# The mask of the forgetful heads: from matmuls to additions on VectorE, with three pieces of the schedule moved

## The chip, the cores and the metric

The kernel runs on one core of a Trainium2 chip. The metric is the device time of one execution in microseconds; the time before is the median of three executions. The core has a matrix engine (TensorE, PE in the profile), two engines for elementwise work and reductions that can read the matrix engine's accumulator banks (VectorE, DVE; ScalarE, ACT), a general engine (GpSimd, POOL) and a sequencer that issues most DMAs (SP).

## What is computed

One layer of a streaming encoder on 1024 tokens of width 1024, all in float32: a normalised input goes through one wide projection into three mixers, whose outputs are gated, added and projected, and then through a gated MLP with a causal convolution.

```python
u = rms_norm(x, norm_mix_g) @ w_in          # latent, forgetting, scan and gate columns
y_a = latent_attention(u_mla) @ w_br_mla    # 8 heads, chunk-causal mask
y_b = forgetting_attention(u_fox) @ w_br_fox
y_c = scan_branch(u_ssm) @ w_br_ssm         # Mamba-2 state-space scan, 16 heads
g = sigmoid(u_gate + b_gate)                # three gates of width 1024
x = x + (g0 * y_a + g1 * y_b + g2 * y_c) @ w_out
x = x + conv_ffn(rms_norm(x, norm_ffn_g), ffn_w_up, ffn_conv_w, ffn_conv_b, ffn_w_down)
```

In forgetting attention the scores of query and key get the difference of two running sums of a forget gate, and keys after the query are masked out one by one:

```python
F = cumsum(log_sigmoid(f_raw + b_f))
s = q @ k.T * scale + F[query] - F[key]
p = softmax(where(key <= query, s, -inf))
```

## The kernel before

A float32 product is computed as three matmuls of a rounded high part and a low remainder (high by high, high by low, low by high). A helper, `split` (line 131), makes the two parts: the high part by a copy on ScalarE, the low one by a subtraction on VectorE.

The work runs in stages: the projections of the latent branch and of the forgetting and z columns (to about 387 us), attention, the scan, the three branch projections, the output projection, and the MLP. Two long lists of work cross the stages:

- **The fill** (`all_fill`, line 1162): the projection of the convolved columns and of the gates, 36 blocks of 48 matmuls (line 1179) on PE. It has no place of its own. `merge(streams, fill_us)` (line 1216) interleaves generators by a planned clock: each yields after a few matmuls with their planned cost, and the stream that is furthest behind its share goes next; `fill_us` says how much fill goes along, with three matmuls counted as 0.65 us. Steps on other engines are put into a queue with `later(us, fn)` (line 1076) and issued when the planned clock passes their due time. PE follows the order that is written out; the other engines' order is planned by a scheduler on that program, except for instructions that `pin` or `keep_in_program_order` ties. What fill is left after the scan is run out at once ahead of the branches.
- **Weight sums of the down projection** (`down_sums`, line 931): the last MLP product uses a scheme with seven block products, for which sums of weight blocks are prepared. Each call loads two tiles by SP, makes four sums on POOL and leaves two stores, which the next call or `down_flush` issues. Six calls are made in the early projections, five in the branches.

Attention (from line 1424): 16 heads, eight latent and then eight forgetting ones, four units each. A unit takes two rows of 128 queries. `score_row` (line 1282) computes the scores of a row in one or two chunks into banks of PSUM (three banks), three matmul passes for latent heads, two for forgetting ones. Then `finish` orders the rest of the row: `last_max` on VectorE (the negated maximum, line 1312, and for two chunks the smaller of two, line 1314), the exponential on ScalarE with its sum (line 1319), sum and reciprocal on VectorE (lines 1324 and 1325), and scaling on POOL (line 1326). The transposes of the probabilities (line 1384), their split and the products with the values (lines 1349 to 1357) come two units later.

The mask of the forgetting heads concerns the last 128 columns of a row. It is one more matmul into the bank of scores, a bf16 identity by a bf16 mask (line 1310), accumulated after the score matmuls. For these heads `finish` is not called in place: it goes into the list `held`, and `merge` or the next row calls it (`flush`), by preference just before the transposes of the values' stream (`tp_next`).

The scan (from line 1465) works on eight chunks of 128 tokens. `ssd_a` transposes the inputs (line 1506), transposes B and multiplies C by B into one bank (lines 1517 and 1519), copies and splits B's transpose (line 1520), makes `cbm` (line 1522) on VectorE from the same bank, and then the decay matrices E: differences by a Relu on ScalarE (line 1538), an exponential (line 1539), a product with `cbm` (line 1540). `ssd_b` makes states and outputs (lines 1548 and 1574) and the norm; `ssd_c` transposes the result (line 1609) and stores it. Fill runs between them, by `FILL_SSD` per chunk and 6.0 us ahead of the first.

The branches (from line 1678): forgetting first, then latent, then scan, each in eight column blocks of 128 (line 1729). A block loads its weights (line 1060) and its gates (line 1720) and splits the weights. The first two inputs of the forgetting branch are loaded into tiles (`ws0`, `ws1`) which the calls of `down_sums` in the branches use later.

Of the kernel before, what the change touches and what calls it, by code (L numbers as in the profile page):

```python
# [11 lines left out]
F32 = mybir.dt.float32  # L12
F32R = mybir.dt.float32r
BF16 = mybir.dt.bfloat16
I32 = mybir.dt.int32
AF = mybir.ActivationFunctionType
# [5 lines left out]
P = 128  # L22
# [20 lines left out]
def block_kernel(ctx: ExitStack, tc: tile.TileContext, x, positions, norm_mix_g, w_in, b_gate,  # L43
# [23 lines left out]
    def const(shape, dt, name):  # L67
        return (cp if name in keep else cp2).tile(shape, dt, name=name, tag=name)

    def scratch(shape, name, dt=F32):  # L70
# [22 lines left out]
    make_identity(nc, ident)  # L93
    identb = const([P, P], BF16, "identb")
    G.tensor_copy(identb, ident)
    ones = const([P, P], F32, "ones")
# [6 lines left out]
                    pattern=[[-1, P]], channel_multiplier=1)  # L103
    mfox = const([P, P], BF16, "mfox")
    G.memset(mfox, 0.0)
# [1176 lines left out]
    def score_row(o, i, pn):  # L1282
        flush()
        n = i + 1
# [6 lines left out]
        for ci, (a, b) in enumerate(chunks):  # L1291
            ps, pl = a_s.get()
            w = max(b - a, 256)
            last = ci == len(chunks) - 1
            for i_, (q_, k_) in enumerate(o.passes):
                T.matmul(ps[:, :w], q_[:, qs], k_[:, a:a + w], start=i_ == 0,  # L1296
                         stop=(o.br == 0 or not last) and i_ == len(o.passes) - 1)
            c = len(o.passes) * w / 2400
            pss.append((ps, pl))
            if not last:  # L1300
                later(c + 0.1, lambda ps=ps, ci=ci, a=a, b=b: pin(V.reduce_max(
                    nmx[:, ci:ci + 1], ps[:, :b - a], axis=AX, negate=True)))
                yield c
# [3 lines left out]
        def finish(t0=0.0):  # L1307

            if o.br == 1:
                T.matmul(ps[:, b - a - P:b - a], identb, mfox, start=False, stop=True)  # L1310
            def last_max():
                V.reduce_max(nmx[:, ci:ci + 1], ps[:, :b - a], axis=AX, negate=True)  # L1312
                if two:
                    V.tensor_tensor(nmx[:, 2:3], nmx[:, 0:1], nmx[:, 1:2], op=ALU.min)  # L1314
# [14 lines left out]

        if o.br == 0:  # L1330
            finish(c)
            yield c
        else:
            held.append(finish)
            yield c + 0.05

# [87 lines left out]
    with ExitStack() as pt__:  # L1424
# [10 lines left out]
        with tc.manual_schedule(engines={mybir.EngineType.PE}):  # L1435
# [6 lines left out]
            for n in range(len(units) + 2):  # L1442
# [11 lines left out]
                if n >= 2:  # L1454
# [4 lines left out]
                    st.append((me[0], cost_v(done[n - 2][1])))  # L1459
                merge(st, FILL_ATT * share)  # L1460
            flush()
# [12 lines left out]
    with ExitStack() as ps__:  # L1474
# [22 lines left out]
        def ssd_a(o, c):  # L1497
# [20 lines left out]
            for g in range(2):  # L1518
                T.matmul(pt[:, 2 + g, :], o.bc[:, g, :], o.bc[:, 2 + g, :], start=True, stop=True)
            split(*o.bT, pt[:, 0:2, :])  # L1520
            split(*o.c_, o.bc[:, 2:4, :])
# [12 lines left out]
            for q in range(4):  # L1534
                E = pool.tile([P, 4, P], F32, name=uid("E"), tag="E", bufs=4)
                for hh in range(4):
                    h = 4 * q + hh
                    A.activation(E[:, hh, :], o.row[:, h, :], AF.Relu, scale=-1.0, bias=cumc[:, c, h:h + 1])
                A.activation(E, E, AF.Exp, scale=-1.0)
                V.tensor_mul(E, E, cbm[:, q // 2:q // 2 + 1, :].to_broadcast([P, 4, P]))  # L1540
                o.E.append(E)
                if q == 1 and c + 1 < NT:
                    split(*o.xdd, xdd)
                yield 0.0
# [71 lines left out]
        with tc.manual_schedule(engines={mybir.EngineType.PE}):  # L1616
# [3 lines left out]
            load_rows(obj[0], 0)  # L1620
            merge([], 6.0)
            grain[0] = 4
# [15 lines left out]
    with ExitStack() as pe_:  # L1638
# [39 lines left out]
        for b, wsrc, nk in ((1, w_br_fox, 4), (0, w_br_mla, 4), (2, w_br_ssm, 8)):  # L1678
# [28 lines left out]
            for j in range(NK):  # L1707
                if (b, j) in ((1, 4), (0, 0), (2, 1), (2, 3), (2, 5)):
                    down_sums(ws_tiles())
                elif (b, j) in ((0, 3), (2, 6)):  # L1710
                    down_flush()
# [502 lines left out]
```

## Time and profile before

| | us |
|---|---|
| median of 3 runs | 2002.59 (2002.17 to 2005.0) |
| the profiled execution's own time | 2003.73 |
| its span, from the first instruction to the last | 2002.0 |
| PE busy | 1977.5 (99% of the span) |
| VectorE busy | 1365.9 (68%) |
| ScalarE busy | 944.5 (47%) |
| GpSimd busy | 651.9 (33%) |

Busy time of PE counts matmuls whose modelled spans overlap, so a full row does not say that it runs at its peak; the distance from one start to the next says what an instruction takes of the queue. A row of the timeline has start, duration, engine, line, operation, output and inputs, shapes, and in brackets the engine's idle time before it with what ended it. A row of the groups has the count, the busy time, the mean duration in ns, and the idle time before. A row of waits has who waited for whom, the total, how often, and the longest. "issue" stands where the profile shows no releaser.

### The profile page before, as it was taken

How to read it: one execution, taken by the hardware profiler on the slowest of the kernel's cores; microseconds unless marked ns; L12 is line 12 of the kernel's file. 1: busy time of each engine (PE TensorE's matmuls, PEld its weight loads, DVE VectorE, ACT ScalarE, POOL GpSimd, SP SyncE). 2: the span in 40 equal slices, each digit the busy share in tenths (PEclk: the TensorE clock that was granted, in tenths of full speed). 3: DMA queues.
4: the chain of work that ended last, by engine and by line, in shares of the span. 5: the costliest groups of instructions: out<-in, count | busy, mean ns of one | idle time of the engine just before them, and what ended most of it. 6: DMA issues, size and time to landing. Idle time of an engine off the chain costs nothing.

```text
span 2002.0 us, 28702 instructions
## 1 busy us (share of the span) xinstructions
PE 1977.5 (99%) x10185; PEld 1676.7 (84%) x10185; DVE 1365.9 (68%) x2345; ACT 944.5 (47%) x1778; POOL 651.9 (33%) x636
## 2 busy tenths in 40 slices
PE   8999999999999999999999999999999999999998
PEld 7989888888888888888888888888888888888887
DVE  7777567267666677656885476568997777666665
ACT  5555323255555556557775132225454444544432
POOL 5133322021212223213331252100764544423764
PEclk9999999999999999999999999999999999999999
DMA  5166857543535444427654786433332211249575
GB/s 178 52 195 210 277 179 224 165 125 105 139 114 145 122 120 133 125 78 238 183 192 139 259 284 202 144 119 107 104 95 90 78 55 53 78 159 337 188 262 185
DMA packets 278265, 312.18 MB, mean 156 GB/s; under 512 B 19197, under 2 KB 209289, under 8 KB 278122
## 3 DMA queue, kind: packets, MB, share of 16 engines
q1 hardware_dynamic: 278120, 310.35, 49.6%
q8 instruction: 80, 1.31, 0.3%
q14 instruction: 63, 0.52, 0.1%
q10 hardware_dynamic: 2, 0.00, 0.0%
HBM read 217.17 MB, written 93.13 MB: 155 GB/s over the span
## 4 chain that ended last, share of the span: by engine, by line
PE 86%; DVE 4%; issue 3%; DMA 3%; POOL 2%; ACT 2%; SPq 1%; ACTq 0%; DVEq 0%; POOLq 0%
PE mm L1179 19%; PE fx L798 9%; PE dn L2161 8%; PE ybr L1729 7%; PE ua L1820 6%; PE uc L1820 5%; PE ud L1820 4%; PE wo L1865 4%; PE s L1296 4%; PE tp L1384 3%; PE ub L1820 2%; PE fxv L188 2%; PE py L1574 1%; PE o L1357 1%; PE ckv L517 1%
## 5 line engine op out<-in xcount | busy, mean ns | idle before, releaser
L1326 POOL TENSOR_SCALAR pm<-pm,rs 128x128 f32<-128x128 f32 (+7 forms) x128 | 105.3, 826 | 413.9 <-DVE rs L1325 290.1
L1179 PE MATMUL mm<-hnh,wh 128*128 128x512 f32 x576 | 236.9, 411 | 0.0
L1179 PE MATMUL mm<-hnh,wl 128*128 128x512 f32 x576 | 226.0, 392 | 0.0
L1179 PE MATMUL mm<-hnl,wh 128*128 128x512 f32 x576 | 225.8, 392 | 0.0
L2161 PE MATMUL dn<-dr,dr 128*128 128x512 f32 x592 | 182.3, 389 | 0.0
L1319 ACT ACTIVATE pm<-s,nmx 128x128 f32<-128x128 f32 (+2 forms) x192 | 110.4, 581 | 64.9 <-DVE nmx L1314 61.4
L2161 PEld LDWEIGHTS dn<-dr,dr 128*128 128x128 f32 x592 | 111.1, 188 | 23.0
L1179 PEld LDWEIGHTS mm<-hnh,wl 128*128 128x128 f32 x576 | 108.1, 188 | 24.6
L1179 PEld LDWEIGHTS mm<-hnl,wh 128*128 128x128 f32 x576 | 108.9, 189 | 15.6
L1179 PEld LDWEIGHTS mm<-hnh,wh 128*128 128x128 f32 x576 | 108.8, 189 | 15.5
L1390 DVE TENSOR_TENSOR ptl<-tp,pth 128x512 fp32r<-128x512 f32 (+1 forms) x160 | 98.4, 633 | 32.8 <-ACT pth L1389 30.7
L1389 ACT ACTIVATE pth<-tp 128x512 fp32r<-128x512 f32 (+1 forms) x160 | 84.8, 555 | 72.6 <-PE tp L1384 72.5
L2161 PE MATMUL dn<-dr 128*128 128x512 f32 x296 | 115.3, 389 | 1.1 <-DVE dY L2178 1.1
L135 DVE TENSOR_TENSOR dr<-dr,dr 128x1024 fp32r<-128x1024 f32 x52 | 75.8, 1465 | 49.1 <-ACT dr L134 47.2
L1729 PE MATMUL ybr<-ah,wl 128*128 128x512 f32 x256 | 99.7, 390 | 1.1 <-DVE wl L135 1.1
L1729 PE MATMUL ybr<-al,wh 128*128 128x512 f32 x256 | 99.8, 390 | 0.0
L1729 PE MATMUL ybr<-ah,wh 128*128 128x512 f32 x256 | 99.7, 389 | 0.0
L134 ACT ACTIVATE dr<-dr 128x1024 fp32r<-128x1024 f32 x52 | 55.1, 1061 | 73.0 <-PE dn L2161 50.0
L1312 DVE TENSOR_REDUCE nmx<-s 128x1 f32<-128x384 f32 (+3 forms) x128 | 65.8, 518 | 32.7 <-PE s L1296 19.1
L134 ACT ACTIVATE wh<-wr 128x1024 fp32r<-128x1024 f32 (+1 forms) x40 | 35.1, 877 | 98.1 <-PE ybr L1729 45.9
L1384 PE MATMUL tp<-ident,pm 128*128 128x128 f32 x576 | 79.8, 273 | 0.6 <-POOL pm L1326 0.6
L135 DVE TENSOR_TENSOR wl<-S,wh 128x1024 fp32r<-128x1024 f32 x42 | 63.2, 1504 | 23.3 <-ACT wh L134 23.3
(531 smaller groups left out, 5782.7 us busy)
## 6 DMA issues: line engine op xcount, KB each, us to landing
dr<-act_d SPq DMA_DIRECT2D x99, 256.0 KB
wr<-in_w_in_dram SPq DMA_DIRECT2D x36, 512.0 KB
g_d<-t SPq DMA_DIRECT2D x24, 512.0 KB
gl<-g_d SPq DMA_DIRECT2D x24, 512.0 KB
wr<-in_ffn_w_up_dram SPq DMA_DIRECT2D x23, 512.0 KB
ws<-in_ffn_w_down_dram SPq DMA_DIRECT2D x22, 512.0 KB
wsum_d<-ws SPq DMA_DIRECT2D x22, 512.0 KB
act_d<-fa SPq DMA_DIRECT2D x22, 512.0 KB
```

The lines of the kernel that those rows point to most:

```text
L134: i = A.activation(h, src, AF.Copy) if he is A else he.tensor_copy(h, src)
L135: return i, le.tensor_sub(l, src, f32(h))
L798: T.matmul(p, a(k), b(k), start=k == 0 and i == 0, stop=k == NK - 1 and i == 2)
L1179: T.matmul(ps, a[:, k, :], b[half][:, k, :], start=(k == 0 and i == 0), stop=(k == NK - 1 and i == 2))
L1319: pss[cj][1][0] = later(t0 + 0.9 + 0.1 * cj, lambda cj=cj, a_=a_, b_=b_: A.activation(p_[:, a_:b_], pss[cj][0][:, :b_ - a_], AF.Exp, bias= ...
L1326: G.tensor_scalar(p_[:, 0:n * P], p_[:, 0:n * P], rs[:, 3:4], 0.0, op0=ALU.mult, op1=ALU.add)
L1384: T.transpose(pt[:, off:off + P], pn[qi][0][:, k * P:k * P + P], ident)
L1389: later(cs + 0.05, lambda th=th, pt=pt, off=off: A.activation(th[:, :off], pt[:, :off], AF.Copy))
L1390: pl[0] = later(cs + 0.6, lambda th=th, tl=tl, pt=pt, off=off: V.tensor_sub(tl[:, :off], pt[:, :off], f32(th[:, :off])))
L1729: T.matmul(pss[half], w_[:, k, :], a_[k][:, hs], start=k == 0 and i == 0, stop=k == nk - 1 and i == 2)
L1820: T.matmul(ps, a, b, start=first and n == 0, stop=n == 11, skip_group_check=not first)
L2161: T.matmul(ps[m], a[:, ts_], b[:, 512:], start=first_ and j == 0 and q == 0, stop=j == NFH - 1 and q == 2, skip_group_check=not first_)
```

## The change

The mask becomes a float32 tile, and the bf16 identity goes. Every row calls `finish` in place, whatever the kind of head; for forgetting heads `last_max` first adds the mask on VectorE to the last 128 columns, in PSUM. (`held` stays in the code and is always empty.) Three places of the schedule change with it. The first two units of attention get 2.0 us more fill each, and the scan's start gets 9.0 us of fill instead of 6.0. In the scan, each difference of a chunk is ordered behind the copy of B's transpose on ScalarE, an order without a semaphore. Two calls of `down_sums` move: from block 4 of the forgetting branch and block 0 of the latent one to blocks 2 and 6 of the forgetting branch; the flush in the latent branch comes at block 2 instead of 3.

```diff
-    identb = const([P, P], BF16, "identb")
-    G.tensor_copy(identb, ident)
...
-    mfox = const([P, P], BF16, "mfox")
+    mfox = const([P, P], F32, "mfox")
...
             for i_, (q_, k_) in enumerate(o.passes):
                 T.matmul(ps[:, :w], q_[:, qs], k_[:, a:a + w], start=i_ == 0,
-                         stop=(o.br == 0 or not last) and i_ == len(o.passes) - 1)
+                         stop=i_ == len(o.passes) - 1)
...
         def finish(t0=0.0):
 
-            if o.br == 1:
-                T.matmul(ps[:, b - a - P:b - a], identb, mfox, start=False, stop=True)
             def last_max():
+                if o.br == 1:
+                    V.tensor_add(ps[:, b - a - P:b - a], ps[:, b - a - P:b - a], mfox)
                 V.reduce_max(nmx[:, ci:ci + 1], ps[:, :b - a], axis=AX, negate=True)
...
-        if o.br == 0:
-            finish(c)
-            yield c
-        else:
-            held.append(finish)
-            yield c + 0.05
+        finish(c)
+        yield c
...
-                merge(st, FILL_ATT * share)
+                merge(st, FILL_ATT * share + (2.0 if n < 2 else 0.0))
...
-            split(*o.bT, pt[:, 0:2, :])
+            b_copy, _ = split(*o.bT, pt[:, 0:2, :])
...
-                    A.activation(E[:, hh, :], o.row[:, h, :], AF.Relu, scale=-1.0, bias=cumc[:, c, h:h + 1])
+                    behind_(A.activation(E[:, hh, :], o.row[:, h, :], AF.Relu, scale=-1.0, bias=cumc[:, c, h:h + 1]),
+                            b_copy)
...
-            merge([], 6.0)
+            merge([], 9.0)
...
-                if (b, j) in ((1, 4), (0, 0), (2, 1), (2, 3), (2, 5)):
+                if (b, j) in ((1, 2), (1, 6), (2, 1), (2, 3), (2, 5)):
                     down_sums(ws_tiles())
-                elif (b, j) in ((0, 3), (2, 6)):
+                elif (b, j) in ((0, 2), (2, 6)):
                     down_flush()
```

## The prediction

> **What bounds the kernel now.** I read the page first: busy shares, then the chain that ended last.
>
> ```profile
> span 2002.0 us, 28702 instructions
> PE 1977.5 (99%) x10185; PEld 1676.7 (84%) x10185; DVE 1365.9 (68%) x2345; ACT 944.5 (47%) x1778; POOL 651.9 (33%) x636
> PE 86%; DVE 4%; issue 3%; DMA 3%; POOL 2%; ACT 2%; SPq 1%; ACTq 0%; DVEq 0%; POOLq 0%
> ```
>
> TensorE is the bound: a microsecond is won only where a matmul leaves its queue or a wait of its queue goes. Next came the busy time by stage (columns: window, its length, then PE, PEld, DVE, ACT, POOL busy) for latent attention (387 to 634 us) and forgetting attention (634 to 886), and then PE's own waits from 386 to 1200 us.
>
> ```profile
> 387.00:634.00 247.00, 243.96 (x1421) 212.99 (x1420) 162.28 (x379) 134.11 (x335) 56.40 (x69) 1.00 0.46 124
> 634.00:886.00 252.00, 251.77 (x1506) 210.67 (x1505) 172.85 (x405) 145.18 (x360) 62.31 (x71) 1.00 0.44 121
> ...
> PE stp L1506 <- issue: 2.5, 2, 1.4
> PE o L1349 <- DVE o L1367: 1.6, 1, 1.6
> PE ybr L1729 <- DVE wl L135: 1.1, 1, 1.1
> PE stp L1506 <- DVE o L1367: 0.9, 1, 0.9
> PE s L1296 <- ACT pm L1319: 0.8, 1, 0.8
> PE stp L1506 <- PE py L1574: 0.8, 1, 0.8
> PE tp L1384 <- POOL pm L1326: 0.6, 1, 0.6
> ```
>
> The forgetting stage leaves PE idle for 0.23 us of 252 at the full granted clock (1.00). So nothing is to be had from its waits, only from its matmuls; the stages around it have 8.3 us of waits in all.
>
> **The change, part by part.** *1. The mask matmuls go.* The mean duration of a mask matmul overlaps its neighbours; what counts is start to start on PE.
>
> ```profile
> L1310 PE MATMUL s<-mfox,identb 128*128 128x128 bf16 x64 | 14.8, 231 | 0.0
> ...
> 762.65 0.23 PE L1310 MATMUL s<-mfox,identb 128*128 128x128 bf16 x1
> 762.69 0.36 PE L1349 MATMUL o<-pth,vv 128*128 128x256 f32 x1
> 762.89 0.22 PE L1354 MATMUL o<-pth,vv 128*64 128x128 f32 x1
> ...
> 770.11 0.28 PE L1349 MATMUL o<-pth,vv 128*128 128x256 f32 x1
> 770.22 0.22 PE L1354 MATMUL o<-pth,vv 128*64 128x128 f32 x1
> ...
> 868.05 0.52 PE L1296 MATMUL s<-qk,qk 128*128 128x384 f32 x2
> 868.41 0.49 PE L1384 MATMUL tp<-ident,pm 128*128 128x128 f32 x3
> ...
> 870.35 0.23 PE L1310 MATMUL s<-mfox,identb 128*128 128x128 bf16 x1
> ...
> 870.83 0.28 PE L1349 MATMUL o<-pth,vv 128*128 128x256 f32 x1
> ...
> 642.08 0.23 PE L1310 MATMUL s<-mfox,identb 128*128 128x128 bf16 x1
> 642.15 1.17 PE L1384 MATMUL tp<-ident,pm 128*128 128x128 f32 x8
> ```
>
> Mask plus value matmul take 0.24 us (762.65 to 762.89); the same value matmul with no mask ahead takes 0.11 (770.11 to 770.22). Mask plus two score matmuls take 0.48 (870.35 to 870.83) against 0.36 (868.05 to 868.41). So the mask costs 0.12 us there: 0.04 of its own and 0.08 by which the matmul behind the bf16 one starts the rest late. Ahead of transposes it costs 0.07 (642.08 to 642.15). By order on PE 24 of the 64 stand ahead of transposes and 40 ahead of other matmuls: 24 x 0.07 + 40 x 0.12 = 6.5 us. The lower bound counts own steps alone: 24 x 0.07 + 40 x 0.04 = 3.3; the upper 64 x 0.13 = 8.3. I take -6.5: PE is idle for 0.23 us in that stage, so nothing else holds it there. [...]
>
> *2. VectorE adds the mask.* Sixty-four additions of 128x128 in the bank of scores. The nearest rows are an operation with one operand from such a bank (cbm) and the rows of ptl at two widths:
>
> ```profile
> L1522 DVE TENSOR_TENSOR cbm<-stp,tri 128x256 f32<-128x256 f32 x8 | 3.3, 413 | 0.0
> L1390 DVE TENSOR_TENSOR ptl<-tp,pth 128x512 fp32r<-128x512 f32 x96 | 65.1, 686 | 17.9 <-ACT pth L1389 16.1
> L1390 DVE TENSOR_TENSOR ptl<-tp,pth 128x384 fp32r<-128x384 f32 x64 | 35.3, 552 | 14.8 <-ACT pth L1389 14.6
> ```
>
> Each 128 columns are 0.134 us (686 - 552), so 128 columns take 0.413 - 0.134 = 0.28 us, and 64 take 17.9 us. VectorE then has 172.85 + 17.9 = 191 us of some 246, 78%. Each sits between a row's scores and its maximum, with the exponentials, sum, reciprocal and POOL's scaling behind it; conv taps and the low halves of transposes queue behind it too. The cover is the order of units: transposes of a unit come two units after its scores, and three banks hold scores. The held finish goes too: scores, transposes and values follow one another as in the latent stage. That stage has the same rule with no mask, and its rows above show 3.0 us of PE waits, 1.4 of them at its start; I take the other 1.6 as the price. Bounds: 0 and, with every addition bare, +17.9.
>
> *3. Two more us of fill in each of the first two units.* PE's waits for ACT pm (0.8) and POOL pm (0.6) are at the stage's start. Fill delays later units against their scores, but it also shifts all conv work against the heads. I take -1.0; bounds -3.0 (all three waits of the stage) and +1.5, as much again.
>
> *4. Nine instead of six us of fill at the scan's start.* The first scan transpose waits 0.9 us for the attention's last output (DVE o). Three more us of matmuls in front cover it: -0.9, bounds -0.9 and 0.
>
> *5. The differences of the scan come behind the copy of B on ScalarE.* Three waits of the next chunk's first transpose (2.5 + 0.8 = 3.3 us) end where VectorE has read the bank for cbm:
>
> ```profile
> 1016.03 0.37 ACT L134 ACTIVATE bTh<-stp 128x256 fp32r<-128x256 f32 x1
> ...
> 1018.36 1.21 DVE L1123 TENSOR_TENSOR wl<-wr,wh 128x1024 fp32r<-128x1024 f32 x1
> 1019.49 0.41 DVE L135 TENSOR_TENSOR bTl<-stp,bTh 128x256 fp32r<-128x256 f32 x1
> 1019.83 0.41 DVE L1522 TENSOR_TENSOR cbm<-stp,tri 128x256 f32<-128x256 f32 x1
> ...
> 1020.34 0.41 PE L1506 MATMUL stp<-ident,t 128*128 128x128 f32 x2 [1.38 <-issue]
> ...
> L1538 ACT ACTIVATE E<-row,strict 128x128 f32<-128x128 f32 x16 | 5.2, 393 | 0.2 <-PE py L1574 0.2
> ```
>
> The copy ends at 1016.40, but bTl starts at 1019.49, queued behind a weight's low half. ScalarE spends 5.2 us on differences from 1007 to 1021 (the last row); those ahead of the copy move behind it, so copy, bTl and cbm can come earlier. Queued behind the tied differences are the exponentials and the py matmuls, which want the four E tiles of a chunk; PE's list of waits names no E, so there is slack, and I charge nothing. I take two thirds of the waits: -2.2; bounds -3.3 and +3.3, as much again for late E.
>
> *6. The fill is used up 2 + 2 + 3 = 7 us of its own count earlier.* Its total is fixed, so it is missing at the end, where it covers the last chunk's norm and the load of the forgetting branch:
>
> ```profile
> 1082.30 5.50 PE mm L1179 x24
> ...
> 1088.23 2.78 PE mm L1179 x12
> ...
> 1091.45 2.77 PE mm L1179 x12
> ...
> 1091.98 2.00 ACT L134 ACTIVATE ah<-ar 128x1024 fp32r<-128x1024 f32 x2
> ```
>
> The code counts 0.65 us per three matmuls, so 7 us are some 32 matmuls; in steps of 12 they leave 12 or 24 of the 48 from 1082.30 on. The branch's first matmul would then come 5.5 to 8.3 us sooner after the last chunk, while its operands (ah, from 1091.98) depend on copies of ScalarE of which I can move only those that wait for the transposes. I take +2.0; bounds 0 (the copies move forward) and +4.
>
> *7. Weight sums of the down projection* move from the latent branch's start into the forgetting branch, two DMAs of SP with them, their stores a block earlier. The one branch wait, 1.1 us for wl, came while POOL made such sums:
>
> ```profile
> 1136.11 0.68 DVE L135 TENSOR_TENSOR wl<-wr,wh 128x512 fp32r<-128x512 f32 x1
> ...
> 1148.78 1.83 DVE L135 TENSOR_TENSOR wl<-wr,wh 128x512 fp32r<-128x512 f32 x1 [0.66 <-ACT wh L134]
> ...
> 1148.79 1.27 POOL L942 TENSOR_TENSOR ws<-ws,ws 128x512 f32<-128x512 f32 x1
> ```
>
> The same split took 0.68 us alone and 1.83 beside the sum. Taken out of there: -1.1. The loads now stand ahead of a block's weights and gates on SP and need the tiles that held the first attention rows, so SP waits for their copies; a block has 5.5 us of matmuls and weights come a block ahead, so nothing is charged. Bounds -1.1 and +1.1, should a second such wait come there. [...]
>
> *8. The identity in bf16 and its POOL copy go, the mask becomes f32:* set up long before 634 us, 0.
>
> Sum: -6.5 + 1.6 - 1.0 - 0.9 - 2.2 + 2.0 - 1.1 = -8.1 us. The profiled execution took 2003.73 us (span 2002.0, 1.7 around it), 1.1 above the median 2002.59; it would become 1995.6, and the median 1994.5.
>
> **The rivals.** *VectorE decides the forgetting stage.* If the additions lie bare between scores and exponentials, part 2 costs 17.9 and not 1.6: 1994.5 + 16.3 = 2010.8. It decides from 8.1 + 1.6 = 9.7 us of bare additions on, that is 54%. For it speaks 78% busy; against it PE's 0.23 us of idling in 252 and the two units between scores and transposes. At three quarters bare (13.4) it gives 2006.3.
>
> *Only the matmul's own step goes* (the slowed neighbour stays, by another switch of types): 3.3 and not 6.5, 1997.7. The rows without a mask in front speak against it.
>
> *The scan's waits stay, and the branch's start opens*: VectorE's queue and not ScalarE held cbm (part 5 gives 0), the missing fill costs 4: 1994.5 + 2.2 + 2.0 = 1998.7. For it speaks bTl's 3 us behind a copy that was done; against it that an earlier copy lets the order change.
>
> *All waits named go and none comes*: -6.5 - 3.0 - 0.9 - 3.3 - 1.1 = -14.8, 1987.8. Against it stands the latent stage with 3.0.
>
> **How the numbers follow.** A measurement here can tell about 0.2% (4 us) from no change. The forecast with small shifts of its terms, 1990 to 1997: 0.50. Own step only, 1997.7: 0.12. Scan waits stay and branch opens, around 1998.7, half of it beyond 1998.6: 0.18. All waits go, 1987.8: 0.13. VectorE decides: 0.07, of which 0.05 beyond 2006.6. Within 0.2% is then 0.09 + 0.02 and some 0.03 of the forecast's edge: 0.14; slower 0.05; faster 0.81. The range leaves out the deepest of the fourth and the last of the third and first cases: 1987 to 2001.
>
> **What would show it.** In the profile after: no bf16 matmul, 64 additions of about 0.28 us on VectorE, and the stage of 252 us shorter by 4 to 6.5 with PE's waits in it below 3 us. The scan's waits of the first transpose (L1506) fall from 4.2 us in all to below 2; the wait for wl in the branches goes; a new one of 1 to 4 us stands at the first ybr matmul. Wrong would make it: transposes waiting for POOL's pm across the forgetting stage, py waiting for E, or the latent stage's waits growing under the shifted fill.

## The result and the profile after

The changed kernel is slower: 2016.76 us (2013.47 to 2022.08) against 2002.38 us of the kernel before, measured beside it; the ratio is 1.0071, 95% interval 1.0055 to 1.0086, or 14.2 us. The forecast was 1994.5 us with 1987 to 2001, so sign and range were both wrong. The profiled execution took 2017.43 us, 13.7 us more than that of before. One run of a_nofill, a kernel of the experiments, took 2806.76 us at a mean granted clock of 0.655 and is left out of the ratios.

From the page of the changed kernel, the span, the busy time by engine and the chain that ended last:

```profile
span 2015.6 us, 28651 instructions
PE 1981.1 (98%) x10121; PEld 1684.3 (84%) x10121; DVE 1381.3 (69%) x2409; ACT 943.8 (47%) x1778; POOL 656.7 (33%) x635
PE 45%; issue 2%; DVE 2%; POOL 1%; ACT 1%; DMA 1%; SPq 0%; ACTq 0%; POOLq 0%; DVEq 0%
```

Sixty-four matmuls have gone from PE, yet its busy time rose by 3.6 us: part of what is left ran at a lower clock, as shown below (mean granted clock 0.995, before 1.000). VectorE has 64 instructions and 15.4 us more.

The stages, cut at the first score matmul of a head, the first scan transpose, and the first ybr, wo and dn matmul. A fill matmul takes 2.78 us / 12 = 0.232 us (the prediction's row at 1088.23), and their total is the same in both kernels, so the last column is the change in length with the change in fill taken off.

| stage | before, us (fill) | after, us (fill) | change net of fill |
|---|---|---|---|
| up to the attention | 389.96 (24) | 389.12 (24) | -0.8 |
| latent attention | 244.29 (546) | 245.29 (564) | -3.2 |
| forgetting attention, 7 head spacings | 216.32 (504) | 221.58 (510) | +3.9 |
| its last head and tail | 52.89 (132) | 53.46 (138) | -0.8 |
| scan | 190.61 (522) | 196.65 (492) | +13.0 |
| branches | 175.96 | 179.19 | +3.2 |
| output, norm, up projection | 515.79 | 515.81 | 0.0 |
| down projection | 216.20 | 214.53 | -1.7 |

The sum is 13.6 us. The scan's row holds PE's wait of 2.4 us for ah, as the cut is the first ybr matmul behind it. The last row goes with a wait of 1.1 us for dY that comes and goes among the kernels here, whatever part of the change they have. PE's own waits after (who waited for whom, total, how often, longest):

```profile
PE s L1294 <- ACT pm L1317: 6.9, 7, 2.4
PE pof L1543 <- DVE hst L1561: 3.7, 1, 3.7
PE stp L1604 <- ACT y L1596: 3.6, 1, 3.6
PE ybr L1724 <- ACT ah L132: 2.4, 1, 2.4
...
PE ybr L1724 <- DVE wl L133: 1.2, 1, 1.2
PE stp L1500 <- issue: 1.0, 1, 1.0
```

The list names the three places. In the forgetting stage the score matmuls now wait for the exponentials to empty their bank. In the scan there are two stalls that the kernel before did not have, while of the waits that the tie was aimed at 1.0 us is left of 3.3 (the tie alone leaves 2.9, as shown below). At the branch's start PE waits for ah.

How a forgetting row gets late, in the timeline of the changed kernel (start, duration, engine, line):

```profile
657.43 0.29 DVE L1309 TENSOR_TENSOR s<-s,mfox 128x128 f32<-128x128 f32 x1
...
658.28 0.55 DVE L1310 TENSOR_REDUCE nmx<-s 128x1 f32<-128x384 f32 x1
...
658.75 0.68 DVE L1384 TENSOR_TENSOR ptl<-tp,pth 128x512 fp32r<-128x512 f32 x1
...
659.35 0.74 DVE L1135 SCALAR_TENSOR_TENSOR t<-t,pc_g,t 128x510 f32<-128x510 f32 x1
...
660.00 0.55 DVE L1384 TENSOR_TENSOR ptl<-tp,pth 128x384 fp32r<-128x384 f32 x1
660.47 0.15 DVE L1312 TENSOR_TENSOR nmx<-nmx 128x1 f32<-128x1 f32 x1
660.72 0.58 ACT L1317 ACTIVATE pm<-s,nmx 128x384 f32<-128x384 f32 x1 [0.65 <-DVE nmx L1312]
...
661.44 0.63 PE L1294 MATMUL s<-w0h,w0l 128*128 128x384 f32 x2 [2.10 <-ACT pm L1317]
```

The addition takes 0.29 us, close to the estimated 0.28. But addition, maximum and the smaller of the two maxima, which the exponentials need, are spread over 3 us of a VectorE without a gap: two differences and a tap stand in between. The next matmul in PE's queue waits 2.10 us for them.

The first stall of the scan, on VectorE and GpSimd:

```profile
953.08 1.91 POOL L1523 TENSOR_TENSOR xdd<-xT,dend 128x1024 f32<-128x1024 f32 x1 [2.33 <-ACT xT L1501]
953.14 2.40 DVE L1560 TENSOR_TENSOR hst<-hst,cdec 128x512 f32<-128x512 f32 x1
...
954.94 2.35 POOL L1525 TENSOR_TENSOR y<-xT,Db 128x1024 f32<-128x1024 f32 x1
...
955.46 2.92 DVE L1519 TENSOR_TENSOR xd<-xT,dt 128x1024 f32<-128x1024 f32 x1
958.30 0.68 DVE L1561 TENSOR_TENSOR hst<-hst,pst 128x512 f32<-128x512 f32 x1
...
959.12 0.77 PE L1543 MATMUL pof<-hsh,Ch 128*128 128x512 f32 x1 [3.71 <-DVE hst L1561]
```

The next chunk's xT is ready just when VectorE is at this chunk's state. The product of hst takes 2.40 us beside GpSimd's xdd and xd 2.92 beside its y, and xd stands ahead of the sum that PE waits for. The second stall, in the same kernel, is GpSimd's queue:

```profile
976.64 1.38 POOL L177 TENSOR_SCALAR rg_t<-yr,rg_v 128x1 f32<-128x1 f32 x1
977.98 2.92 POOL L1523 TENSOR_TENSOR xdd<-xT,dend 128x1024 f32<-128x1024 f32 x1
980.90 0.26 POOL L178 TENSOR_SCALAR yr<-rg_t,yr 128x1 f32<-128x1 f32 x1
...
981.12 1.90 POOL L1525 TENSOR_TENSOR y<-xT,Db 128x1024 f32<-128x1024 f32 x1
983.01 1.31 POOL L177 TENSOR_SCALAR rg_t<-yr,rg_v 128x1 f32<-128x1 f32 x1
...
985.92 1.12 PE L1604 MATMUL stp<-ident,y 128*128 128x128 f32 x4 [3.62 <-ACT y L1596]
```

Two big products of the next chunk cut into the short steps of this chunk's inverse root, on which ScalarE's scaling of y waits, and on that PE. Behind each of the two stalls came a second price. Windows of the changed kernel around the first (the third number from the end is the mean granted clock):

```profile
957.50:958.00 0.50, 0.00 (x0) 0.00 (x0) 0.50 (x1) 0.00 (x0) 0.00 (x0) 0.76 0.00 0
958.00:964.50 6.50, 5.38 (x18) 4.63 (x19) 6.50 (x10) 3.55 (x9) 0.00 (x0) 0.50 0.36 97
964.50:965.00 0.50, 0.50 (x4) 0.41 (x3) 0.50 (x2) 0.50 (x3) 0.00 (x0) 0.92 0.96 290
```

By the means of the first and the last window the clock is at half from 957.76 to 964.58, 6.8 us, and 5.5 us of that come after the stall has ended at 959.12: some 2.7 us more. The changed kernel has four such stretches (from 787.1, 957.8, 985.1 and 1107.9), where the kernel before has none ahead of its last microseconds. Half of what each has left behind its wait is 1.7, 2.7, 3.0 and 1.7 us: an estimated 9 of the 13.7 us between the two profiled executions are the clock's.

### The profile page after: what moved, and what is told of

The parts are those of the page before. It is cut to its first block, busy times and chain, and to the rows that moved or that the text cites. A ratio compares the mean times of both kernels' runs of the same rounds, so it can differ in the third digit from the quotient of the medians.

```text
span 2015.6 us, 28651 instructions
## 1 busy us (share of the span) xinstructions
PE 1981.1 (98%) x10121; PEld 1684.3 (84%) x10121; DVE 1381.3 (69%) x2409; ACT 943.8 (47%) x1778; POOL 656.7 (33%) x635
## 4 chain that ended last, share of the span: by engine, by line
PE 45%; issue 2%; DVE 2%; POOL 1%; ACT 1%; DMA 1%; SPq 0%; ACTq 0%; POOLq 0%; DVEq 0%
PE dn L2156 10%; PE ybr L1724 7%; PE ua L1815 6%; PE uc L1815 5%; PE ud L1815 4%; PE wo L1860 4%; PE mm L1177 4%; PE ub L1815 2%; PE py L1569 1%; DMA ar<-att_d 1%; PE pof L1543 0%; DVE wl L133 0%; PE pt L1767 0%; DMA wsum_d<-ws 0%; PE stp L1604 0%
```

## The experiments

All start from one of the two kernels. "us" is the ratio less one, times 2002.4. Forgetting stage: from its first score matmul to the first transpose of the scan. The stages are those of the one profiled execution, fill included; in e_fill2 and e_pin_fill2 it took 6.6 and 5.4 us more than the kernel's median, so their stages show more than a typical execution has.

| kernel | ratio to before (95%) | us | forgetting stage | scan | branches |
|---|---|---|---|---|---|
| before | | | 269.2 | 190.6 | 176.0 |
| after | 1.0071 (1.0055 to 1.0086) | +14.2 | 275.0 | 196.7 | 179.2 |
| e_mask: VectorE adds the mask | 1.0040 (1.0027 to 1.0053) | +8.0 | 275.8 | 191.0 | 175.8 |
| e_fill: both fill changes | 1.0017 (1.0008 to 1.0026) | +3.4 | 270.9 | 187.5 | 177.5 |
| e_tie: differences behind the copy | 1.0034 (1.0022 to 1.0047) | +6.8 | 269.2 | 197.6 | 175.9 |
| e_down: weight sums | 0.9999 (0.9989 to 1.0008) | -0.2 | 269.3 | 190.5 | 176.1 |
| e_nomask: as e_mask, mask left out | 0.9977 (0.9967 to 0.9986) | -4.6 | 265.6 | 191.1 | 174.6 |
| e_held: as e_mask, still held | 1.0033 (1.0022 to 1.0043) | +6.6 | 276.6 | 191.1 | 174.9 |
| e_pin: as e_mask, some order kept | 0.9997 (0.9988 to 1.0007) | -0.6 | 269.8 | 191.0 | 176.7 |
| e_chain: as e_mask, other order | 1.0020 (1.0010 to 1.0031) | +4.0 | 273.3 | 190.8 | 175.8 |
| e_twice: as e_mask, twice | 1.0098 (1.0082 to 1.0114) | +19.6 | 287.9 | 191.0 | 175.8 |
| e_fill2: 2.0 us twice, alone | 1.0059 (1.0045 to 1.0073) | +11.8 | 268.1 | 202.1 | 182.0 |
| e_fill9: 9.0 for 6.0, alone | 1.0036 (1.0024 to 1.0048) | +7.2 | 270.9 | 194.2 | 177.5 |
| e_back: e_fill2, taken back | 0.9996 (0.9987 to 1.0005) | -0.8 | 269.4 | 190.5 | 178.4 |
| e_fill_tie: fill and tie | 1.0046 (1.0032 to 1.0060) | +9.2 | 270.8 | 195.3 | 179.5 |
| e_tie_hst: tie, another order | 1.0043 (1.0028 to 1.0058) | +8.6 | 269.2 | 198.6 | 175.9 |
| a_notie: after without the tie | 1.0052 (1.0037 to 1.0067) | +10.4 | 276.4 | 188.2 | 181.3 |
| a_nofill: after without fill | 1.0077 (1.0063 to 1.0092) | +15.4 | 275.7 | 198.0 | 177.1 |
| e_pin_fill2: e_pin and e_fill2 | 1.0080 (1.0065 to 1.0095) | +16.0 | 272.9 | 201.9 | 176.4 |
| e_chain_back: e_chain and e_back | 1.0017 (1.0008 to 1.0026) | +3.4 | 274.1 | 190.7 | 176.0 |

### The four parts alone

e_mask is the change of mask, `last_max` and `finish` without its other parts; the others are these lines:

```diff
# e_fill
-                merge(st, FILL_ATT * share)
+                merge(st, FILL_ATT * share + (2.0 if n < 2 else 0.0))
-            merge([], 6.0)
+            merge([], 9.0)
# e_tie
+                    behind_(A.activation(E[:, hh, :], ...), b_copy)
# e_down
+                if (b, j) in ((1, 2), (1, 6), (2, 1), (2, 3), (2, 5)):
+                elif (b, j) in ((0, 2), (2, 6)):
```

> Part 1 and 2 alone: mask on VectorE, finish in place, nothing else moved. Theory 1 (VectorE's queue costs the forgetting stage its gain; the scan's loss comes from the tie): the seven head spacings of the forgetting stage sum to about 220 us as in the changed kernel (216 before), score matmuls wait some 7 us for ScalarE's exponentials, the scan keeps its small waits, and the whole is about 2004 to 2008. Rival A (the stage is only disturbed by the fill's shifted phase): the stage shrinks to about 211 and the whole to about 1996. Rival B (the shorter stage alone shifts the scan into its two long waits): the scan loses some 10 us here too, 2014 or more.

> Part 3 and 4 alone: 2.0 us more fill in each of two units, 9.0 ahead of the scan. Theory 1: the latent stage's waits fall from 3.0 to about 0.7 us, the scan keeps waits of 3 us, the first branch matmul waits up to 3 us; the whole 1999 to 2003. Rival (the shifted fill brings the scan's two long waits with a halved clock behind them): two waits of over 3 us in the scan, the whole 2010 or more.

> Part 5 alone: the differences of the scan ordered behind the copy of B on ScalarE. Theory 1 (the tie makes VectorE and POOL collide on the state and norm steps): two waits of 3 to 4 us in the scan with the granted clock near 0.5 behind them, the whole about 2013. Rival (the tie helps as forecast and the long waits come from elsewhere): the scan's 3.3 us of waits for cbm fall to about 1, the whole about 2000.

> Part 7 alone: weight sums moved to blocks 2 and 6 of the forgetting branch. If the sums are what costs the branches their 3 us: the branches take 179 us instead of 176 and the whole is about 2005. If it is the missing fill ahead of the branches: the wait of 1.1 us for wl goes and the whole is about 2001.

Alone the parts cost 8.0, 3.4, 6.8 and -0.2 us, 18.0 in all against 14.2 together. Three of four are losses, each in its own stage: the mask in the forgetting stage (+6.6), the tie in the scan (+6.9), the fill by PE's wait of 2.4 us for ah at the branch's start and one of 2.0 for a load in the scan. The sums move nothing that can be measured; the wait for wl at the branch's blocks stays at 1.0 us. That wait was not theirs: in the changed kernel the split of wl takes 0.69 us (at 1159.31, with no work of GpSimd beside it), and PE waits 1.2 us for it all the same, since VectorE comes to it only behind two steps for al.

The two longest of PE's waits with the mask alone, from the attention on, and then with the tie alone, within the scan:

```profile
PE o L1343 <- DVE o L1361: 6.3, 5, 1.6
PE s L1294 <- ACT pm L1317: 5.3, 11, 0.9
```

```profile
PE pof L1549 <- DVE hst L1567: 5.2, 2, 4.2
PE stp L1506 <- issue: 2.9, 2, 1.9
```

So the tie alone makes one long stall, where the first theory had two, and leaves 2.9 us of the 3.3 that it was aimed at. The larger wait of these, in the timeline:

```profile
1000.86 0.38 ACT L134 ACTIVATE bTh<-stp 128x256 fp32r<-128x256 f32 x1
...
1006.78 0.41 DVE L135 TENSOR_TENSOR bTl<-stp,bTh 128x256 fp32r<-128x256 f32 x1
...
1007.63 0.63 PE L1506 MATMUL stp<-ident,t 128*128 128x128 f32 x4 [1.86 <-issue]
```

The copy is early, but bTl starts 5.5 us behind it, in VectorE's queue. Summed over the eight chunks bTl starts 16.8 us behind the copies, and 17.5 in the kernel before: for these waits VectorE's queue and not ScalarE's held cbm, which is what the third rival of the prediction said.

### The forgetting stage: busy time or order?

```diff
# e_nomask: from e_mask; masked scores stay as they are
-                    V.tensor_add(ps[:, b - a - P:b - a], ps[:, b - a - P:b - a], mfox)
# e_held: from e_mask
-        finish(c)
-        yield c
+        if o.br == 0:
+            finish(c)
+            yield c
+        else:
+            held.append(finish)
+            yield c + 0.05
# e_pin: from e_mask; each behind what was written down before it on VectorE
+                    pin(V.tensor_add(...)); pin(V.reduce_max(...)); pin(V.tensor_tensor(..., op=ALU.min))
```

> As e_mask, but the mask is left out altogether: no matmul and no addition, finish in place (the last 128 columns of forgetting rows go unmasked). Theory 2 (the additions, and what VectorE puts between them and the maximum, cost the stage): the seven head spacings fall to about 212 us, with waits of about 1 us, and the whole to about 1996. Rival (it is the order: finish in place instead of held): waits of some 8 us stay, spacings of about 219, the whole 2006 or more.

> As e_mask, but finish stays held for forgetting heads as in the kernel before; only the matmul turns into an addition. Theory 2: the waits stay at some 8 us, spacings about 220, the whole about 2009. Rival (order): waits below 1 us, spacings about 211, the whole about 1996.

> As e_mask, but addition, maximum and smaller of two of the forgetting rows are tied into the written order of VectorE, so that the planner cannot put a conv tap or low halves between them that come later in the program. Theory 2 with the gap between addition, maximum and minimum as its place: waits of the stage fall from 10 to about 2 us, spacings to about 213, the whole to about 1999. Rival (VectorE simply has too much to do): waits stay near 10 us, the whole 2008 or more.

e_nomask leaves the last 128 columns of the forgetting rows unmasked. It is 4.6 us faster than before, not the 6.5 that the forecast gave to the removal. The seven head spacings are 3.5 us shorter though they hold 1.0 us more waits (1.19 against 0.21, the shortest counted too), so 56 mask matmuls took an estimated 4.5 us, 0.081 us each, and 64 of them 5.2. The additions then cost the stage 275.8 - 265.6 = 10.2 us, and PE's waits of 0.15 us or more in it grow by nearly as much, from 0.7 to 10.3. Holding `finish` or not changes little (276.6), so it is not the call in place that costs. Keeping the written order takes 6 of the 10 back (PE's waits in the stage are 4.5 us, between the two theories), so a part of the price looked like order; the next two runs test that.

```diff
# e_chain: from e_mask; differences, taps, outputs, first maxima, sums of heads on VectorE
+    row_min = [None]
+    def past(ins):
+        if row_min[0] is not None:
+            behind_(ins, row_min[0])
+        return ins
...
+                row_min[0] = i_ if o.br == 1 else None
# e_twice: from e_mask
+                    V.tensor_add(ps[:, b - a - P:b - a], ps[:, b - a - P:b - a], mfox)
```

> Mask added by VectorE and finish in place, nothing else of the change; and on VectorE the differences of the transposed weights, the taps, the outputs and the weight differences of the fill, the first maxima and the sums of the heads are queued behind the smaller-of-two (or the only maximum) of the forgetting row last written down. Theory 1 (the additions themselves are cheap, their price is what the planner puts between the last maximum and the smaller of the two, on which the exponentials wait): forgetting stage of seven spacings 215 to 217 us in place of 220.8, waits of TensorE for pm under 3 us, ratio 0.999 to 1.001. Theory 2 (the work that was in between is itself needed by TensorE and waits now instead): 219 us or more, with waits for ptl, o or mm, ratio 1.003 or more.

> Mask by VectorE alone (parts 1 and 2), with each of the 64 additions done twice: 18 us more of VectorE's time, order as the planner makes it. Theory 1 (VectorE has stretches of some us without idle time, where the exponentials, the sums of the heads and the differences all wait for their turn, so each addition there counts): forgetting stage of seven spacings 226 to 232 us in place of 220.8, ratio 1.007 to 1.010. Theory 2 (the addition itself is hidden and only the order that the planner made around it cost): 219 to 223 us, ratio 1.003 to 1.005.

Putting everything else behind the smaller-of-two gives 2.5 us of the 10 back. The exponentials are not waited for less: beside the rows of e_mask above, the waits for pm are 5.9 us in place of 5.3, and those for o, which was passed over, 5.0 in place of 6.3. The seven spacings (220.1 us) are the second theory's, the waits are neither's. PE's waits with e_chain, first; then with the mask added twice:

```profile
PE s L1300 <- ACT pm L1324: 5.9, 8, 2.1
PE o L1350 <- DVE o L1368: 5.0, 5, 1.6
```

```profile
PE s L1294 <- ACT pm L1318: 16.2, 16, 1.6
PE o L1344 <- DVE o L1362: 5.1, 4, 1.6
```

A second addition per row costs 12.1 us more: the dose doubles the loss, as the first theory said (the seven spacings take 231.6 us). By their own rows the additions take 18.7 us once and 37.5 twice, so as the planner orders them they are paid at between half and two thirds of their time; the order of e_pin hides more of it. VectorE's busy share of the stage does not tell this. The windows of the whole stage, without a mask, with it added once and twice:

```profile
635.00:901.00 266.00, 263.69 (x1539) 225.48 (x1537) 180.13 (x414) 151.90 (x371) 64.08 (x71) 1.00 0.45 125
```

```profile
634.00:910.00 276.00, 265.25 (x1540) 225.44 (x1539) 197.48 (x477) 153.59 (x371) 66.51 (x72) 1.00 0.44 120
```

```profile
632.00:920.00 288.00, 266.32 (x1539) 224.84 (x1538) 209.74 (x542) 153.58 (x371) 65.67 (x71) 1.00 0.42 115
```

VectorE is at 68%, 72% and 73% over the stage. But it works in bursts. Five microseconds of before, and the same five of e_mask:

```profile
664.00:669.00 5.00, 5.00 (x32) 4.20 (x32) 4.57 (x9) 2.81 (x6) 2.32 (x1) 1.00 0.83 215
```

```profile
664.00:669.00 5.00, 5.00 (x32) 4.22 (x31) 5.00 (x10) 3.01 (x5) 3.07 (x1) 1.00 0.78 167
```

There VectorE had 0.43 us of slack before, and two additions of 0.28 us fall into that stretch. That such stretches set the price is a reading that no run tested: in the five us up to the end of each of the 16 waits of PE in e_mask's stage, VectorE was idle for 0.23 to 1.49 us, 0.92 at the median. Nor do the runs part the addition's own step in each row's chain from the place that it takes in VectorE's queue.

### The fill

```diff
# e_back: 2.0 us more in two units, taken back over the thirty that follow
+                merge(st, FILL_ATT * share + (2.0 if n < 2 else -4.0 / 30 if n < 32 else 0.0))
```

e_fill2 and e_fill9 are the two lines of e_fill, one each.

> The kernel before with only the 2.0 us of extra fill in the first two units of the latent stage; the scan's opening keeps its 6.0 us. Theory 1 (the two halves of the fill change act apart): the latent stage keeps the gain it had with both (244.29 us with 546 fill matmuls to about 245.3 with 564, waits of TensorE 3.0 to 0.7 us, net 3.2 us less), the branches stay at 176 us, and the time is 2 to 3 us below before, ratio about 0.9987. Theory 2 (the stock of 1728 fill matmuls is fixed, so what the latent stage takes is missed at the end of the scan): the first ybr waits some 2.4 us for ah as with both, the clock behind it falls, the branches take 177 to 179 us, and the ratio is 0.9995 to 1.0015.

> The kernel before with only the 9.0 us of fill in place of 6.0 at the opening of the scan. Theory 1 (the loss of both together, 4.1 us in the median, comes from here): latent stage as before (244.3 us), a wait of about 2 us for the load from xbc_d or for the first copies of the scan, branches 177 us or more, ratio 1.002 to 1.003. Theory 2 (the loss comes from fill that the latent stage took): scan within 1 us of before once its fill is taken off, branches 176 us, ratio 0.9995 to 1.0005.

> The kernel before with 2.0 us more fill in each of the first two units of the latent stage, taken back in equal parts (0.13 us) over the thirty units that follow. Theory 1 (early fill closes waits of the latent stage, and what it lost alone came from a shifted order at the opening of the scan): latent stage net of fill 114 to 115 us in place of 117.3, scan as in before (190.6 us, no wait for the load from xbc_d), branches 176 us, ratio 0.998 to 0.999. Theory 2 (the gain of the latent stage is fill that other places lack): net 116 us or more, waits return later in the stage, ratio 0.9995 to 1.001. Theory 3 (any shift of the fill reorders the scan's loads): latent gain as in theory 1 and a scan of 195 us or more, ratio over 1.001.

Neither half is harmless: 11.8 and 7.2 us alone, 3.4 together. Neither theory gave such times. With e_fill2 the latent stage gains as with both (net 114.6 us against 117.8), and then the scan loses 15.7 net of fill. What SyncE's queue and PE do there in e_fill2:

```profile
904.20 2.24 SPq L1482 DMA_DIRECT2D row<-cum_d  x2
...
915.16 0.80 SPq L1482 DMA_DIRECT2D row<-cum_d  x2
...
916.47 0.43 SPq L1492 DMA_DIRECT2D t<-xbc_d  x1
...
924.34 1.09 PE L1506 MATMUL stp<-ident,t 128*128 128x128 f32 x4 [5.52 <-DMA t<-xbc_d]
```

and in the kernel before:

```profile
906.60 1.23 SPq L1482 DMA_DIRECT2D row<-cum_d  x2
...
907.88 0.67 SPq L1492 DMA_DIRECT2D t<-xbc_d  x1
...
917.41 0.60 PE L1506 MATMUL stp<-ident,t 128*128 128x128 f32 x4
```

The shift of the fill changes the order on SyncE. The load of the next chunk's xs now stands behind a third pair of row loads, which waits 4.0 us for ScalarE to be done with a row buffer, and is issued at 916.47 and not at 907.88. PE needs it at 918.8 and stalls for 5.5 us, and the granted clock is 0.50 from 920.9 to 927.7. Three more waits for scan transposes are 5.9 us (two of 2.5 before), and half clock comes again for 3.4 us from 1013.0 and for 6.8 from 1105.2. By its mean granted clock of 0.994 the profiled execution lost an estimated 12 us of its span of 2018.7, some 2 of them while PE waited: 10 of the 16.7 us by which it is longer than that of before. With 9.0 us of fill at the opening PE comes there later and waits 2.0 us. Fill of 9.0 alone gave two other stalls (3.1 and 2.3 us for scan transposes), neither of them the load that was expected: again another order.

e_back asked whether the latent gain is real. Its stage is 117.5 us net of fill, against 117.8: the gain has gone with the fill, and the kernel is equal to before (0.9996), as the second theory said. So early fill only moves work into the latent stage's waits. It pays if the place it is taken from does not miss it, and the scan and the branch's start do.

### The scan, and the parts in company

```diff
# e_tie_hst: e_tie, and on VectorE xd and the difference of xdd behind the last sum of hst
+            past_hst(V.tensor_mul(o.xd, xv, hb(dt, c)))
+                    past_hst(split(*o.xdd, xdd)[1])
```

e_fill_tie is e_fill and e_tie; a_notie and a_nofill are the changed kernel without the one or the other; e_pin_fill2 and e_chain_back join two edits shown above.

> The tie alone, and on VectorE the next chunk's xd and the difference of its xdd queued behind the last sum of hst written down. Theory 1 (the price of the tie is that order at one place, doubled by the halved clock behind the stall): no wait of TensorE for hst over 1.5 us, scan 190 to 193 us in place of 197.6, ratio 0.999 to 1.001. Theory 2 (the price is that all scan differences come late, and VectorE and GpSimd slow each other wherever they meet): a stall of the same size moves to pst, py or stp, scan 195 us or more, ratio 1.002 to 1.004.

> Both fill changes and the tie, no mask by VectorE, no moved sums. Alone they cost 4.1 and 7.5 us. Theory 1 (they overlap: the tie moves the row loads, which wait for E, behind the load of the second chunk on SyncE's queue, so the wait for xbc_d goes; fill covers part of the tie's late steps): 6 to 8 us above before, about 2009, scan 196 us with no wait for a load. Theory 2 (no overlap; what is counted twice in the changed kernel lies with the mask): 11 to 12 us above before, about 2014, with both the wait for xbc_d and the waits for hst.

> The changed kernel without the tie of the scan's differences (part 5 undone). Theory 1 (the tie makes the two long waits and the halved clock): both go, the scan is some 10 us shorter, and the whole falls from 2016 to 2006 or so. Rival (in the changed kernel the shifted fill makes them): at least one wait of over 3 us stays and the whole is 2012 or more.

> The kernel after with both fill changes undone: mask by VectorE, tie and moved weight sums stay. Alone, mask, tie and fill cost 8.0, 7.5 and 4.1 us, together 14.4 and not 19.6, so about 5 us are counted twice. Theory 1 (what is counted twice lies between the fill and the other two: with late sums in scan and forgetting stage, early fill costs nothing more): the sum of mask and tie, 15 to 16 us above before, about 2018, and branches of 176 us. Theory 2 (it lies between mask and tie): 10 to 11 us above before, about 2013.

> Addition, maximum and minimum of the forgetting rows kept in their written order on VectorE, and 2.0 us of fill in the first two units; no tie, no 9.0 us, no moved sums. Theory 1 (causes add up): the pinned kernel's 0.9997 and 3 us less in the latent stage, ratio 0.998 to 0.999, about 1999; forgetting stage of seven head spacings about 216 us with 3 to 4 us of waits. Theory 2 (the fill that the latent stage takes is missed later): 1.000 to 1.002, with a wait of 2.4 us for ah at the first ybr and branches above 177 us.

> The queued order of the first kernel of this call with the fill of the second. If both first theories hold, forgetting stage 215 to 217 us, latent net 114 to 115 us, scan as in before: ratio 0.997 to 0.999. If the fill shifts the forgetting rows as it did the pinned kernel (216.1 to 222.2 us there): 1.002 to 1.005.

Queuing xd and xdd behind the state takes the stall at hst away and gives nothing: PE's longest wait of e_tie_hst is now

```profile
PE stp L1617 <- ACT y L1609: 6.1, 1, 6.1
```

the one for y that the changed kernel has too. So the price of the tie is not one unlucky order. The reading that fits, argued from these rows: with the differences late, the next chunk's products meet this chunk's state and root on VectorE and GpSimd, and one of them stalls PE. That the tie causes these stalls and the mask does not, e_fill_tie shows: 3.7 us for hst and 3.6 for y, as in the changed kernel, with no mask by VectorE. Which of the meetings could be avoided together was not tried.

e_fill_tie also shows a gain of the tie in company: SyncE issues the load ahead of the third pair of rows again, and the wait for it is gone. Fill and tie cost 9.2 us, 1.0 less than one by one. In the changed kernel the fill costs nothing: without it 15.4 us, about the sum of mask and tie (14.8), with it 14.2. The tie still costs 3.8 us there (10.4 without it): the scan is 8.5 us shorter without it, but forgetting stage and branches are 1.4 and 2.1 longer.

The two joined kernels do not mend. e_chain_back has seven spacings of 220.9 us, where 215 to 217 were hoped for. e_pin's order does not survive the shift of the fill: with e_fill2 its seven head spacings go from 216.1 to 222.2 us, with the same waits for pm as in the changed kernel (6.9 us in 7, the longest 2.4). No kernel here is measurably faster than before and complete: e_back, e_pin and e_down are equal to it.

## Why the prediction was wrong

The step that failed is the second: the additions were priced at 1.6 us, and they cost 10.2. By the runs of the parts alone, against the terms of the sum:

| step | forecast | measured | off by |
|---|---|---|---|
| 1 and 2, mask by VectorE | -4.9 | +8.0 | 12.9 |
| 5, tie | -2.2 | +6.8 | 9.0 |
| 3, 4 and 6, fill | +0.1 | +3.4 | 3.3 |
| 7, weight sums | -1.1 | -0.2 | 0.9 |
| counted twice | | -3.8 | -3.8 |

The sum is 22.3 us, and so far was the forecast off (14.2 + 8.1).

**1, the matmuls.** The mechanism held: no bf16 matmul is left, and the 64 cost more than their own steps (3.3 us). The size was an estimated 5.2 us and not 6.5. The price of 0.12 us ahead of other matmuls was read at two places and taken for 40; by the run without a mask it is an estimated 0.081 on the mean over all 64.

**2, the additions: the step that failed first.** The duration (0.295 us on the mean, for an estimated 0.28) was right. The price was taken from the latent stage, which runs in place without a mask and waits 1.6 us, as if the order of units covered the rest. The runs showed 10.2 us, 57% of the estimated 17.9. The rival "VectorE decides the forgetting stage" named this mechanism and its threshold of 54%, and got a chance of 0.07, because 0.23 us of PE idling in 252 was read as cover. That number says that nothing was late before; it does not say by how much each row was early, and VectorE's queue had 0.43 us to spare in the five us shown above. By how much the rows were early was not measured, so why 57% and not more or less of the additions was paid stays open.

**3 and 4, the fill.** The waits named did go: latent attention gained 3.2 us net of fill, and the wait for the last output is off the list. What the working lacked was that a shift of the fill reorders SyncE's queue in the scan (the load 8.6 us later), though it did say that the fill shifts other work.

**5, the tie.** Two things failed. The waits named stayed, 2.9 of 3.3 us with the tie alone, since bTl waited for VectorE; that only 1.0 is left in the changed kernel takes the fill as well (e_fill_tie has the same 1.0, and e_fill, without the tie, waits 1.4 for that transpose behind PE's own). And the sentence that failed is "there is slack, and I charge nothing": it looked only for waits for E. E was not waited for; xd, the state and the inverse root of other chunks came to meet on VectorE and GpSimd. The upper bound, +3.3, was half of what came; the clock behind the stall, an estimated 1.9 us in e_tie's scan, was no part of it.

**6, the end of the fill.** Right in place and cause: twelve fill matmuls are left ahead of ybr, and PE waits 2.4 us for ah. The size was some 4 us and not 2.0, at the upper bound: to the wait come the branches, 1.5 us longer with the fill alone and 3.2 in the changed kernel, 2.1 of which go with the fill (a_nofill has 177.1). A stretch of half clock behind the wait, 3.4 us from 1093.7 in e_fill, is an estimated 1.4 of the 1.5.

**7, the sums.** The wait for wl was put down to them by one meeting of two rows. It stayed at 1.0 to 1.2 us with the sums elsewhere, in the changed kernel even where no work of GpSimd slowed the split: two things beside each other were taken for cause and effect.

## What to carry to other kernels

Where one engine is never idle, ask of each edit that loads another how early its results are where it is most pressed, not how busy it is over the stage; leaving the suspected work out and adding it twice are cheap tests of its price. A planner that issues from modelled times answers every small shift with other orders on all queues, so parts that look free (fill a bit earlier, an order without a wait) can cost more than the step they serve, and their prices do not add. Price a stall of TensorE with the slow stretch that may follow it, an estimated 1.7 to 3.0 us in the changed kernel, and read which waits a part alone removes before it is credited with their going.

## What the runs showed of the hardware

The granted clock of TensorE fell to half for stretches of one length or two, 3.4 or 6.8 us, leaving the last microseconds of the kernels aside. Five waits of PE of 3.6 to 6.1 us were followed by 6.8 us (3.7 and 3.6 in the changed kernel, 5.5 in e_fill2, 4.2 in e_tie, 6.1 in e_tie_hst) and one of 3.1 in e_fill9 by 3.4. Seven of 2.1 to 2.7 us were followed by 3.4 us (2.39 and 2.38 in the changed kernel, 2.4 for ah in e_fill, 2.7 in e_fill2, 2.10, 2.4 and 2.5 in e_pin_fill2) and five of 2.0 to 2.8 us by none (2.10 in the changed kernel at 661, 2.0 in e_fill, 2.3 in e_fill9, 2.1 in e_chain, 2.8 in the kernel before at 39). The stretches began 1.2 to 4.2 us after PE ran dry. Which came was not settled by the length of the wait alone: one of 1.7 us for ah in e_fill2, with 0.8 for al just behind it, was followed by 6.8 us, and those of 1.6 us in the kernel before (at 538) and in the changed kernel (at 39) by none. The clock also makes most of the spread among executions of the changed kernel: the six, from 2013.47 to 2022.08 us, times their mean granted clocks, 0.997 to 0.993, come to 2007.3 to 2008.0 us each. The windows behind the wait of 2.39 us that ended at 786.30, in the changed kernel:

```profile
787.00:788.00 1.00, 1.00 (x4) 0.81 (x3) 1.00 (x5) 0.00 (x0) 0.48 (x1) 0.55 0.00 0
788.00:790.00 2.00, 2.00 (x6) 1.54 (x6) 0.72 (x2) 1.15 (x4) 0.75 (x1) 0.50 0.00 0
790.00:791.00 1.00, 1.00 (x8) 0.95 (x7) 0.86 (x2) 0.34 (x3) 0.00 (x0) 0.75 0.00 0
```

Many short waits cost no clock in e_twice: it had 1.00 over its whole forgetting stage (632 to 920 us), with 16 waits for pm of 16.2 us in all and of up to 1.6 us each.

VectorE and GpSimd took longer beside each other in the changed kernel's scan: 2.40 us for the product of hst and 2.92 for xd in the rows above, which began while a product of GpSimd ran, where hst's eleven other products took 0.68 to 0.69 and the seven other xd 1.21 to 1.23. GpSimd's xdd took 2.92 to 2.95 in the four chunks where xd began 0.05 us ahead of it, the second stall's among them, and 1.91 in the three others.
